# A hybrid decoder trunk: one part of layer 0's modulation summed on GpSimd during the state-space tiles

## The chip, the cores and the metric

The kernel runs on one core of a Trainium2 chip. Its engines work side by side, each through its own queue in order: TensorE (PE, with PEld for weight loads), VectorE (DVE), ScalarE (ACT), GpSimd (POOL) and SyncE (SP, which here only issues DMAs). They wait for one another through semaphores. The metric is the device time of one execution in microseconds, less is better.

## The reference

Two layers on a sequence of 256 tokens with 2048 channels. Each layer has a token mixer and a feed-forward part, and each of the two has three modulation vectors, made from one conditioning vector c:

```python
c_act = jax.nn.silu(c)
for i in range(DEPTH):
    mod = c_act @ ada_w[i] + ada_b[i]          # 2048 x (6 * 2048)
    sh_m, sc_m, gt_m, sh_f, sc_f, gt_f = [m[:, None, :] for m in jnp.split(mod, N_MOD, axis=-1)]
    h = x * (1.0 + sc_m) + sh_m
    y = s5_mixer(h, ...) if i % 2 == 0 else conv_mixer(h, ...)
    x = layer_norm(ALPHA * x + (1.0 + gt_m) * y, ln_g[i, 0], ln_b[i, 0])
    h = x * (1.0 + sc_f) + sh_f
    y = swiglu_ffn(h, ffn_w_gu[i], ffn_w_down[i])
    x = layer_norm(ALPHA * x + (1.0 + gt_f) * y, ln_g[i, 1], ln_b[i, 1])
```

Layer 0's mixer is a state-space scan (S5): 128 groups of 16 channels with 64 complex states each, then gelu and a gated projection with a 2048 x 4096 matrix. Layer 1's is a causal convolution between two projections. The six modulation parts of a layer are counted 0 to 5 below (sh_m, sc_m, gt_m, sh_f, sc_f, gt_f). Parts 0 and 1 of layer 0 are needed ahead of the scan, part 2 (the gate) when the mixer's output is added to x, parts 3 and 4 ahead of the feed-forward part, part 5 behind it. Each part is a product of c_act with 2048 rows of 2048 columns, 16 MB of weights.

## The kernel before

**Preparation** (0 to about 56 us): the scan's matrices are made, mostly on DVE and POOL.

**The state-space tiles** (about 56 to 254 us, the loop over ct in the kernel's function): 16 tiles of 128 channels. For tile ct, `tables` makes a table of powers (tile `tab`; two buffers): ACT copies the first half, POOL makes the second with four operations (`xt`, `yt`, two into `tab`, L350) from tile 2 on. `drive` brings the tile's input into a PSUM tile `pin` by matmuls (L413). `scan` on DVE multiplies `pin` by the table into `x` and `pin` (L430), scans (L442), carries the state over (L449 to L455), and turns back into `pc` and `psn` (L430). `read_out` makes y by 64 matmuls (L478). `gelu` is done in three steps between the scan's (DVE L1289, L1293, L1298; ACT), the last of which splits the result into a high and a low half, the low one on POOL (`h`, L1300). For every quarter of the tiles POOL also makes matrices ahead of time (`matrices`, L313: `mu`, `qb`, `qc`).

**Modulation blocks on PE** (`ada_block`, `ada_units`): in the first stage the modulation is made on PE. A block is one part and 512 columns; a unit is a quarter of it: one load of 1 MB on SP's queue into a buffer `raw`, and four matmuls (L605), whose total is turned (`adat`) and added up at the end of the block. Fourteen blocks, 56 units, go that way: parts 0 and 1, part 2, and the first half of part 3. The list `plan` says how many units go into each tile. Their order on PE is that of the code (`manual_schedule`); the other engines' order is set by a scheduler when the program is built. The buffers `raw` are five in this stage: four of the pool `rawp`, and one of a pool of its own.

**The rest of the modulation on DVE** (`AdaQueue`): from the end of the tiles on, DVE adds the rows of a part up itself: a 1 MB load `rawa`, then `acc = row * c_act[k] + acc` (L673, L675), and at the end of a part PE sums over the partitions (`total`, L683) and turns the result (`turned`). `rate` says how many steps fall to one weight unit of the dense part.

**The dense part** (from 254 us): gated projection, feed-forward, convolution, feed-forward. Weights of float32 are split into a high half (ACT, `whi`, L806) and a low half (DVE, `wlo`, L807), and PE multiplies (L856). `Later` puts small pieces of work off by a number of weight units. At the start of the gated projection, twelve `later.put` calls bring the units of `ada_block` that are left. The tail of tile 15 (`s5_end`) is done inside it.

Of the kernel before, what the change touches and what calls it, by code (L numbers as in the profile page):

```python
# [484 lines left out]
def kernel(  # L485
# [16 lines left out]
    def aux(name):  # L502
        return auxp.tile([P, 512], F32, tag="aux", name=name)
# [114 lines left out]

    class AdaQueue:
# [44 lines left out]
        def add(self, layer, j, b0, k, r):  # L664
            nb = 4 - b0
            rows, n = 4 // nb, 512 * nb
            if k == 0:
                self.acc = sp_ada.tile([P, D], F32, tag="adaacc", name="adaacc")
            acc = self.acc[:, :n]
            for i in range(rows):  # L670
                kk = rows * k + i
                if kk == 0:
                    nc.vector.tensor_scalar(out=acc, in0=r[:, 0], scalar1=c_act[:, 0:1], scalar2=None, op0=MUL)  # L673
                else:
                    nc.vector.scalar_tensor_tensor(out=acc, in0=r[:, i], scalar=c_act[:, kk:kk + 1], in1=acc, op0=MUL, op1=ADD)  # L675
            if kk < NCH - 1:
                return
            h = 32 * nb

            def total():  # L680
                ps = auxp.tile([P, 512], F32, tag="ada", name="adar", bufs=1)
                for b in range(nb):
                    nc.tensor.matmul(ps[32 * b:32 * b + 32, :], ones[:, 0:32], acc[:, 512 * b:512 * b + 512], start=True, stop=True)  # L683
                part = tp.tile([P, 512], F32, tag="adas", name="adas", bufs=1)
                nc.scalar.copy(out=part[:h], in_=ps[:h])
                later.put(1, lambda: turned(part))

            def turned(part):
                tr = aux("adat")
                for b in range(4):  # L690
                    nc.tensor.transpose(tr[:, b * h:(b + 1) * h], part[:h, b * P:(b + 1) * P], ident[:h, :h])
                nc.vector.scalar_tensor_tensor(
                    out=mod[layer][:, j, 4 * b0:].rearrange("p (b c) -> p c b", c=4),
                    in0=tr[:, :4 * h].rearrange("p (c b r) -> p c b r", b=nb, r=32)[:, :, :, 0],
                    scalar=plus_one(j), in1=ab_col[layer][:, 16 * j + 4 * b0:16 * j + 16].rearrange("p (b c) -> p c b", c=4),
                    op0=ADD, op1=ADD)

            later.put(1, total)


# [507 lines left out]
    parts = [(j, q) for q in range(4) for j in (0, 1)] + [(2, q) for q in range(4)] + [(3, 0), (3, 1)]  # L1208
# [108 lines left out]
    const2 = wp = ln_col = wtap = fold32 = row_of = None  # L1317
    with tc.manual_schedule(engines={mybir.EngineType.PE}):
        ada_units(3)
        for ct in range(-1, NCH):  # L1320
# [33 lines left out]
            while turns:  # L1354
                between()
    pin_ctx.close()
# [8 lines left out]
    ada = AdaQueue([(0, 3, 2), (0, 4, 0), (0, 5, 0)] + [(1, j, 0) for j in range(5)] + [(1, 5, 2)])  # L1365
# [43 lines left out]
    with mctx:  # L1409
        sp = mctx.enter_context(tc.tile_pool(name="s", bufs=1, reuse_waits="tile"))  # L1410
        sp_ada = mctx.enter_context(tc.tile_pool(name="ada", bufs=1, reuse_waits="tile"))
        stats = Stats("ln00", sp)
        ada.rate = 0.9
        for k in range(12):
            later.put(1 + k, lambda: ada_units(1))
# [14 lines left out]
        for i in range(8):  # L1430
# [6 lines left out]
            ada.hold = i == 6  # L1437
            if i == 0:
                later.put(10, load_vectors)
# [155 lines left out]
```

## Time and profile before

| what | value |
|---|---|
| median of 3 runs | 2387.75 us (2384.18 to 2388.4) |
| the profiled execution | 2382.7 us |
| its span | 2380.8 us |
| granted clock of TensorE, mean | 0.98 |
| busy: PE, DVE, ACT, POOL | 2279.4, 1665.8, 1021.3, 209.3 us |

The profile's page gives the span in 40 equal slices of 59.5 us. A digit is the busy share of a slice in tenths, PEclk the clock that TensorE was granted:

```profile
PE   5878899999999999999999999899999999999999
DVE  8999688787777677777985554788755444454564
POOL 4433000110000000000031111402000000000000
PEclk7998899999999999999999999999999999999999
```

The first four slices are the preparation and the state-space tiles, with DVE at 9 and PE at 8; the rest is the dense part, with PE at 9 throughout.

### The profile page before, as it was taken

The numbers are of one execution on the slowest core, as the hardware profiler recorded it, in microseconds if no ns is written. First come the engines' busy times: TensorE is split into PE (matmuls) and PEld (weight loads), VectorE is DVE, ScalarE is ACT, GpSimd is POOL, SyncE is SP. The second block draws the span as 40 slices with busy tenths as digits, with TensorE's granted clock in tenths as the row PEclk, the third lists the DMA queues.
The fourth block names the chain that finished last, engine by engine and source line by source line (L and its number), as shares of the span: only waits on it lengthen the run. The fifth ranks groups of instructions, "written<-read, shape, count | busy, mean of one in ns | idle before, by whom it ended". The sixth has DMA issues, their size and how long they took to land.

```text
span 2380.8 us, 34205 instructions
## 1 busy us (share of the span) xinstructions
PE 2279.4 (96%) x13997; PEld 1814.0 (76%) x13997; DVE 1665.8 (70%) x1850; ACT 1021.3 (43%) x1255; POOL 209.3 (9%) x217
## 2 busy tenths in 40 slices
PE   5878899999999999999999999899999999999999
PEld 2444588978888888888886677688888888888888
DVE  8999688787777677777985554788755444454564
ACT  3665233564343333433454332547343433334343
POOL 4433000110000000000031111402000000000000
PEclk7998899999999999999999999999999999999999
DMA  9877899678898889888744654675875555555542
GB/s 288 274 257 226 298 338 331 204 242 316 297 320 308 308 305 315 305 308 305 279 147 165 211 182 146 230 267 163 273 244 185 192 186 188 189 184 193 183 162 98
DMA packets 373330, 572.15 MB, mean 240 GB/s; under 512 B 17171, under 2 KB 267331, under 8 KB 358579
## 3 DMA queue, kind: packets, MB, share of 16 engines
q1 hardware_dynamic: 372742, 569.53, 70.5%
q8 instruction: 109, 1.79, 0.3%
q0 software_dynamic: 192, 0.37, 0.1%
q14 instruction: 47, 0.39, 0.0%
q10 hardware_dynamic: 240, 0.08, 0.0%
HBM read 567.83 MB, written 2.10 MB: 239 GB/s over the span
## 4 chain that ended last, share of the span: by engine, by line
PE 81%; DVE 9%; issue 5%; ACT 2%; POOL 2%; DMA 1%; DVEq 0%; SPq 0%; POOLq 0%; ACTq 0%
PE acc L856 69%; PE acc L860 4%; PE conv L1491 2%; PE turned L872 2%; PE spread L1481 1%; DVE pin L442 1%; POOL h L954 1%; PE y L478 1%; DVE x L430 1%; DVE pc L430 1%; DVE pin L430 1%; ACT whi L806 1%; DVE psn L430 1%; DMA raw<-in_ada_w_dram 1%; DVE wlo L807 1%
## 5 line engine op out<-in xcount | busy, mean ns | idle before, releaser
L807 DVE TENSOR_TENSOR wlo<-raw,whi 128x2048 fp32r<-128x2048 f32 x344 | 790.8, 2299 | 542.2 <-ACT whi L806 541.8
L806 ACT CAST whi<-raw 128x2048 fp32r<-128x2048 f32 x344 | 655.0, 1904 | 832.1 <-PE acc L856 608.8
L856 PE MATMUL acc<-whi,h 128*128 128x512 f32 x3648 | 900.4, 396 | 9.3 <-ACT whi L806 8.0
L856 PEld LDWEIGHTS acc<-whi,h 128*128 128x128 f32 x3648 | 681.1, 189 | 168.8 <-issue 11.5
L856 PE MATMUL acc<-wlo,h 128*128 128x512 f32 x1824 | 464.0, 391 | 1.0 <-DVE wlo L807 1.0
L856 PEld LDWEIGHTS acc<-wlo,h 128*128 128x128 f32 x1824 | 342.4, 188 | 76.8 <-DVE wlo L807 1.4
L856 PE MATMUL acc<-whi,f 128*128 128x512 f32 x1248 | 300.5, 391 | 0.0
L675 DVE SCALAR_TENSOR_TENSOR adaacc<-rawa,c_act,adaacc 128x2048 f32<-128x2048 f32 (+1 forms) x135 | 284.5, 2108 | 0.4
L856 PEld LDWEIGHTS acc<-whi,f 128*128 128x128 f32 x1248 | 233.0, 188 | 48.9 <-ACT whi L806 0.8
L856 PE MATMUL acc<-wlo,f 128*128 128x512 f32 x624 | 156.4, 389 | 0.0
L856 PEld LDWEIGHTS acc<-wlo,f 128*128 128x128 f32 x624 | 117.1, 188 | 24.3
L1470 POOL TENSOR_TENSOR lw<-fold,wtap 128x1024 f32<-128x1024 f32 x16 | 41.8, 2619 | 894.9 <-PE acc L860 710.5
L605 PE MATMUL ada<-raw,c_rep 128*32 128x512 f32 x512 | 75.0, 664 | 17.2 <-DMA raw<-in_ada_w_dram 17.2
L954 POOL TENSOR_TENSOR h<-hf,h 128x512 fp32r<-128x512 f32 x24 | 48.2, 2017 | 325.8 <-ACT h L953 318.6
L1179 ACT ACTIVATE fsg<-acc 128x256 f32<-128x256 f32 x84 | 31.9, 380 | 103.0 <-PE acc L856 102.9
L860 PEld LDWEIGHTS acc<-h,whi 128*128 128x128 f32 x512 | 61.1, 188 | 10.1 <-DVE h L1520 3.1
L860 PE MATMUL acc<-h,whi 128*128 128x256 f32 x512 | 65.1, 281 | 3.6 <-DVE h L1520 1.4
L1125 POOL CAST lnmh<-lno 128x2 fp32r<-128x2 f32 x1 | 0.2, 183 | 713.4 <-DVE lno L65 713.4
L1491 PE MATMUL conv<-vs,lw 128*32 128x256 f32 x1024 | 61.4, 381 | 0.0
L478 PE MATMUL y<-pc,mc 128*32 128x128 f32 x512 | 26.9, 322 | 26.6 <-DVE pc L430 26.6
L1491 PEld LDWEIGHTS conv<-vs,lw 128*32 128x32 f32 x1024 | 33.0, 110 | 25.2 <-issue 4.7
L1180 DVE TENSOR_TENSOR fsg<-acc,fsg 128x256 f32<-128x256 f32 x84 | 35.3, 420 | 19.9 <-ACT fsg L1179 19.8
(329 smaller groups left out, 1907.7 us busy)
## 6 DMA issues: line engine op xcount, KB each, us to landing
raw<-in_ffn_w_gu_dram SPq DMA_DIRECT2D x352, 512.0 KB, 4.5
rawa<-in_ada_w_dram SPq DMA_DIRECT2D x128, 1024.0 KB, 5.6
raw<-in_ffn_w_down_dram SPq DMA_DIRECT2D x88, 1024.0 KB, 5.2
raw<-in_ada_w_dram SPq DMA_DIRECT2D x64, 1024.0 KB, 7.1
raw<-in_s_w_glu_dram SPq DMA_DIRECT2D x64, 512.0 KB, 5.9
raw<-in_cv_w_pw_dram SPq DMA_DIRECT2D x64, 512.0 KB, 4.8
raw<-in_cv_w_pw_dram SPq DMA_DIRECT2D x16, 1024.0 KB, 6.3
X<-in_x_dram SPq DMA_DIRECT2D x8, 256.0 KB, 7.8
```

What stands on the lines that cost most here:

```text
L430: v.tensor_tensor(out=o, in0=i, in1=bc(t[:, k, a::2], 1, 4), op=MUL)
L478: nc.tensor.matmul(y[rr, o:o + HALF].rearrange("p (s c) -> p s c", s=2), self.cols(ct, ids[mi], p), src[:, p % 2, :, r, p // 2], start=Fal ...
L605: nc.tensor.matmul(acc[32 * k:32 * k + 32, :], c_rep[:, 4 * u + k, :], r[:, k, :], start=u == 0, stop=u == 3)
L675: nc.vector.scalar_tensor_tensor(out=acc, in0=r[:, i], scalar=c_act[:, kk:kk + 1], in1=acc, op0=MUL, op1=ADD)
L806: m1 = nc.scalar.copy(out=self.hi[:, :kn], in_=r[:, :kn])
L807: m2 = nc.vector.tensor_tensor(out=self.lo[:, :kn], in0=r[:, :kn], in1=self.hi[:, :kn].bitcast(F32), op=SUB)
L856: nc.tensor.matmul(acc[bank].rearrange("p a b -> p (a b)"), x[:, bank * HALF:(bank + 1) * HALF], wt[:, k], start=first, stop=end)
L860: nc.tensor.matmul(acc[bank][:, i], wt[:, k, m * P:(m + 1) * P], x, start=first and i == 0, stop=end and i == 1)
L872: nc.tensor.transpose(b[:, o:o + HALF], u[t][:, c0 + k * P:c0 + (k + 1) * P], ident)
L954: nc.gpsimd.tensor_tensor(out=hl[:, s2], in0=h, in1=hh[:, s2].bitcast(F32), op=SUB)
L1470: nc.gpsimd.tensor_tensor(out=lw, in0=fold32.unsqueeze(1).unsqueeze(1).broadcast_to([P, 4, CONV_G, 32]), in1=bc(wtap[:, :, 4 * ch:4 * ch + ...
L1491: nc.tensor.matmul(acc[32 * q:32 * q + 32, :], lw[:, q, g, :], vs[:, q, 4 * g:4 * g + SEQ], start=g == 0, stop=g == CONV_G - 1)
```

## The change

Part 2 (the gate) goes neither to PE nor to DVE now. A new class `Gate` has POOL add it up during the state-space tiles: in every tile one row block of 128 x 2048 (1 MB) is loaded by a DMA that POOL issues itself, into a buffer of `rawp`; POOL multiplies it by its column of c_act in place, and adds it to `gate` (the first one is written to `gate` at once). There are 16 of them. `gate.add()` and then `gate.load()` stand at the end of the loop's body, so a load stands one turn of the loop ahead of its addition. The fifth buffer for blocks is given up; its room holds `gate`. PE's 56 units go to parts 0, 1, 3 and the first half of 4. DVE's queue begins at the second half of part 4, 16 rows shorter, and begins only after the first of the eight gated projections (rate 0 there, then 0.6 instead of 0.9); the units left over from the tiles begin at the fifth weight unit instead of the first. The final sum over the partitions (`total`, `turned`) becomes a function `column_sums`, which both use. `gate_end` does it for the gate.

```diff
-    parts = [(j, q) for q in range(4) for j in (0, 1)] + [(2, q) for q in range(4)] + [(3, 0), (3, 1)]
+    parts = [(j, q) for q in range(4) for j in (0, 1)] + [(3, q) for q in range(4)] + [(4, 0), (4, 1)]
...
+    class Gate:
+        def __init__(self, acc):
+            self.k, self.held, self.acc = 0, [], acc
+
+        def load(self):
+            if self.k < NCH:
+                r = rawp.tile([P, 4, 512], F32, tag="raw", name="rawg").rearrange("p a b -> p (a b)")
+                nc.gpsimd.dma_start(r, ada_w[0, self.k * P:(self.k + 1) * P, 2 * D:3 * D])
+                self.held.append((self.k, r))
+                self.k += 1
+
+        def add(self):
+            if self.held:
+                k, r = self.held.pop(0)
+                nc.gpsimd.tensor_scalar(out=r if k else self.acc, in0=r, scalar1=c_act[:, k:k + 1], scalar2=None, op0=MUL)
+                if k:
+                    nc.gpsimd.tensor_tensor(out=self.acc, in0=r, in1=self.acc, op=ADD)
...
-    raws[:] = [rawp] * 4 + [more.enter_context(tc.tile_pool(name="raw5", bufs=1))]
+    gate = Gate(more.enter_context(tc.tile_pool(name="gate", bufs=1, side="right")).tile([P, D], F32, name="gate"))
...
-                    raws[:] = [rawp]
-                    more.close()
                     s5.keep_ctx.close()
...
             while turns:
                 between()
+            gate.add()
+            gate.load()
...
-    ada = AdaQueue([(0, 3, 2), (0, 4, 0), (0, 5, 0)] + [(1, j, 0) for j in range(5)] + [(1, 5, 2)])
+    ada = AdaQueue([(0, 4, 2), (0, 5, 0)] + [(1, j, 0) for j in range(5)] + [(1, 5, 2)])
...
-        sp_ada = mctx.enter_context(tc.tile_pool(name="ada", bufs=1, reuse_waits="tile"))
-        ada.rate = 0.9
+        gate_total, gate_turned = column_sums(0, 2, 0, gate.acc)
+
+        def gate_end():
+            nonlocal sp_ada
+            gate_total(aux("adar"))
+            later.put(2, gate_turned)
+            more.close()
+            sp_ada = mctx.enter_context(tc.tile_pool(name="ada", bufs=1, reuse_waits="tile"))
+
+        later.put(1, gate_end)
         for k in range(12):
-            later.put(1 + k, lambda: ada_units(1))
+            later.put(5 + k, lambda: ada_units(1))
...
             ada.hold = i == 6
+            ada.rate = 0.6
```

The scheduler sets where the new operations stand on POOL. Before, this stood in POOL's queue around the tables of tiles 7 to 9 (the number behind `tab` is the tile, `h` is the low half of a gelu):

```order
L1300 TENSOR_TENSOR h_132<-gl_1519,h_132 128x256
L350 TENSOR_TENSOR xt_1578<-tab7_1576,wt_363 128x256
L350 TENSOR_TENSOR yt_1579<-tab7_1576,wt_363 128x256
L350 TENSOR_TENSOR tab7_1576<-xt_1578,yt_1579 128x4x32 x2
L1300 TENSOR_TENSOR h_132<-gl_1674,h_132 128x256
L350 TENSOR_TENSOR xt_1728<-tab8_1726,wt_363 128x256
L350 TENSOR_TENSOR yt_1729<-tab8_1726,wt_363 128x256
L350 TENSOR_TENSOR tab8_1726<-xt_1728,yt_1729 128x4x32 x2
```

In the changed kernel, from the ninth load on (`rawg` is the gate's buffer, L1318 its load, L1325 the scaling and L1327 the addition), the same engine does:

```order
L1318 DMA rawg_1890<-in_ada_w_dram 128x2048
L1305 TENSOR_TENSOR h_132<-gl_1700,h_132 128x256
L1325 TENSOR_SCALAR rawg_1890<-rawg_1890,c_act_125 128x2048
L1327 TENSOR_TENSOR gate_486<-rawg_1890,gate_486 128x2048
L350 TENSOR_TENSOR xt_1758<-tab8_1756,wt_363 128x256
L350 TENSOR_TENSOR yt_1759<-tab8_1756,wt_363 128x256
L350 TENSOR_TENSOR tab8_1756<-xt_1758,yt_1759 128x4x32 x2
L1318 DMA rawg_2058<-in_ada_w_dram 128x2048
L1305 TENSOR_TENSOR h_132<-gl_1862,h_132 128x256
L1325 TENSOR_SCALAR rawg_2058<-rawg_2058,c_act_125 128x2048
L1327 TENSOR_TENSOR gate_486<-rawg_2058,gate_486 128x2048
L350 TENSOR_TENSOR xt_1929<-tab9_1927,wt_363 128x256
```

Between two tables there stand a load, the scaling that waits for this load, and the addition; a load is issued behind the addition of the load before it. In other tiles (3, 5, 6, 10, 14) the tables stand between the load and the scaling.

On PE the end of the tiles before (`y` is the read-out of tiles 14 and 15, L605 are modulation units):

```order
L413 MATMUL pin<-uh,lz_455 128x2x64 x8
L612 MATMUL adat<-ident,adas 128x128 x4
L605 MATMUL ada<-raw,c_rep 32x512 x4
L468 MATMUL y<-u,bd_458 128x129
L605 MATMUL ada<-raw,c_rep 32x512 x8
L478 MATMUL y<-pc,mc_453 32x128 x16
L478 MATMUL y<-psn,mc_453 32x128 x16
L605 MATMUL ada<-raw,c_rep 32x512 x4
```

and after the change (L627 and L634 are the gate's sum over the partitions and its transposes):

```order
L413 MATMUL pin<-uh,lz_455 128x2x64 x8
L612 MATMUL adat<-ident,adas 128x128 x4
L605 MATMUL ada<-raw,c_rep 32x512 x4
L468 MATMUL y<-u,bd_458 128x129
L627 MATMUL adar<-gate,ones 32x512 x4
L634 MATMUL adat<-ident,adas 128x128 x4
L468 MATMUL y<-u,bd_456 128x129
L478 MATMUL y<-pc,mc_453 32x128 x16
L478 MATMUL y<-psn,mc_453 32x128 x16
L605 MATMUL ada<-raw,c_rep 32x512 x4
```

The gate's total stands ahead of the read-out of tile 14, and three modulation units less stand ahead of the dense part; they follow inside it.

More of the change, by code (lines that the diff above doesn't have):

```diff
@@ L677, in add @@
                 return
[L678 to L698, printed above, removed]
+            total, turned = column_sums(layer, j, b0, acc)
+            later.put(1, lambda: (total(auxp.tile([P, 512], F32, tag="ada", name="adar", bufs=1)), later.put(1, turned)))
     def inverse_std(v, y, hv, t):
@@ L1315, in start_dense @@
             ready.append(Unit(wp, s5_w_glu[0], 4 * u, 4, [(0, 256), (D, 256)]))
-    const2 = wp = ln_col = wtap = fold32 = row_of = None
+    const2 = wp = sp_ada = ln_col = wtap = fold32 = row_of = None
     with tc.manual_schedule(engines={mybir.EngineType.PE}):
```

19 lines of the change are left out of this document (added).

## The prediction

> **What bounds the kernel now.** I read the time by stages first (busy time of each engine in each stretch), then VectorE's groups in the first stage, then single tiles on the timeline.
>
> ```profile
> 60.00:235.00 175.00, 140.42 (x2133) 80.94 (x2135) 165.35 (x358) 110.87 (x318) 64.47 (x113) 0.92 0.76 253
> 235.00:260.00 25.00, 14.84 (x114) 9.39 (x106) 19.29 (x31) 1.69 (x4) 0.72 (x1) 0.61 0.97 328
> 260.00:300.00 40.00, 39.67 (x231) 29.45 (x230) 25.45 (x22) 14.67 (x14) 1.27 (x1) 1.00 0.83 278
> 300.00:440.00 140.00, 140.00 (x704) 115.66 (x703) 121.56 (x118) 60.03 (x61) 0.00 (x0) 1.00 0.92 316
> 500.00:1180.00 680.00, 680.00 (x3092) 557.27 (x3091) 517.35 (x365) 270.58 (x215) 0.00 (x0) 1.00 0.87 308
> ```
>
> Columns: stretch, length, busy us of PE, weight load, DVE, ACT, POOL (with counts), granted clock, DMA share, GB/s. Two machines stand one behind the other. From 60 to 235 us, the state-space tiles, DVE is busy 165 of 175 us and PE is not full. From 260 on PE is full, at a granted clock of 1.00, while DVE has room (517 of 680 us). So the 16 column additions that the change takes from DVE's modulation queue in the dense part buy nothing there: PE sets that time. What the change can win or lose lies ahead of 260 us.
>
> ```profile
> L442 DVE TENSOR_TENSOR_SCAN pin<-rho,pin 128x256 f32<-128x256 f32 x60 | 41.4, 689 | 0.8
> L430 DVE TENSOR_TENSOR x<-pin,tab 128x512 f32<-128x512 f32 x32 | 21.3, 679 | 5.0 <-PE pin L413 5.0
> ```
>
> VectorE's groups of the tile stage: 32 products x for 16 tiles, with 5.0 us idle once, at the start. One tile costs DVE about 12 us. Its first product reads the tile's table (tab), and this table comes from POOL:
>
> ```profile
> 210.62 1.28 DVE L430 TENSOR_TENSOR x<-pin,tab 128x512 f32<-128x512 f32 x2
> 217.90 0.68 DVE L430 TENSOR_TENSOR x<-pin,tab 128x512 f32<-128x512 f32 x1
> 222.05 1.28 DVE L430 TENSOR_TENSOR psn<-pin,tab 128x512 f32<-128x512 f32 x2
> 228.22 0.68 DVE L430 TENSOR_TENSOR x<-pin,tab 128x512 f32<-128x512 f32 x1
> ```
> ```profile
> 218.43 0.73 POOL L1300 TENSOR_TENSOR h<-gl,h 128x256 fp32r<-128x256 f32 x1 [4.05 <-ACT h L1299]
> 223.97 0.61 POOL L350 TENSOR_TENSOR xt<-tab,wt 128x256 f32<-128x256 f32 x1 [4.80 <-ACT tab L358]
> 224.54 0.61 POOL L350 TENSOR_TENSOR yt<-tab,wt 128x256 f32<-128x256 f32 x1
> 225.23 0.88 POOL L350 TENSOR_TENSOR tab<-xt,yt 128x128 f32<-128x128 f32 x2
> 226.05 0.88 POOL L1378 DMA_DIRECT2D rt<-in_cv_w_dw_dram  x1
> ```
>
> The timeline of tiles 13 to 15. Tile 13's psn ends at 223.3 and frees a table buffer, tile 15's table is done at 226.1, and x of tile 15 starts at 228.2. So the table has **2.1 us of slack**, though POOL idles 4 to 5 us ahead of each of its jobs. Idle POOL is not free POOL: what is put there must not be in the way when the table falls due.
>
> **The change, part by part.** *POOL* gets per tile a 1 MB load that it issues itself, a scaling (tensor_scalar, 128x2048) and an addition (tensor_tensor, 128x2048). Neither shape is in the trace. The nearest rows:
>
> ```profile
> L313 POOL TENSOR_TENSOR qc<-mu,mu x12: 720/728/902, 51.3 to 126.4; 128x256 f32<-128x256 f32 x12
> L1530 POOL TENSOR_TENSOR hf<-hf,V x7: 1272/1293/3330, 1506.1 to 1528.8; 128x512 f32<-128x512 f32 x7
> L1470 POOL TENSOR_TENSOR lw<-fold,wtap x16: 1966/2066/4020, 1203.7 to 1467.8; 128x1024 f32<-128x1024 f32 x16
> masks.py:199 POOL TENSOR_SCALAR_AFFINE_SELECT ident<-ident 128x128 f32<-128x128 f32 x1 | 0.3, 295 | 0.1
> L189 POOL MEMSET mb<- 128x512 f32 x2 | 1.1, 535 | 0.0
> ```
>
> Addition: from 728 ns at 256 to 1293 at 512 is 565 ns for 256 elements, so 1293 + 6 x 565 = 4.7 us at 2048; doubling the 1024 row's minimum gives 3.9. I take **4.6** (range 3.9 to 4.7). Scaling has one input: four 512 memsets are 2.1 us (no input at all), the 128-element select gives 16 x 295 = 4.7 with its fixed part counted sixteen times. By the slope of a two-input operation (565/256 = 2.2 ns) a 128-element one has some 0.45 us, the select 0.3, so one input costs about half: **2.3** (range 1.8 to 4.7).
>
> ```profile
> raw<-in_ada_w_dram SPq DMA_DIRECT2D x37, 1024.0 KB, 5.9
> rt<-in_cv_w_dw_dram POOLq DMA_DIRECT2D x1, 128.0 KB, 8.3
> ```
> ```profile
> DMA to landing us min/median/max: 4.8/5.6/8.6
> ```
>
> Landing of a load: 1 MB from SP's queue takes 5.9 us in these tiles, from POOL's queue even 128 KB took 8.3; the last row is rawa, 1 MB in the same rows of 8 KB, over the whole run. POOL's issue occupies it for 0.88 us. I take **6.5** from issue to landing (range 4.8 to 8.3).
>
> Now the order. In the changed order POOL does for tile 8, in a row: issue load 8, h, scale 8, add 8, tables of tile 8, issue load 9, h, scale 9, and so on. Load 9 is issued behind add 8, and scale 9, which waits for that load, stands ahead of the tables of tile 9. So the landing is not hidden behind earlier work; it is a wait in the middle of POOL's queue, and behind it stand tables for which DVE waits. Per tile of this form: 6.5 + 2.3 + 4.6 + 2.1 (tables: 0.61 + 0.61 + 0.88) = **15.5 us against DVE's 12**. In tiles where the tables stand inside the landing it is 13.4 and a little.
>
> The whole chain on POOL, counted off its new order from the issue of load 0 to the tables of tile 15: 15 landings that nothing else on POOL fills (load 2's is filled by an addition and a table), 16 scalings, 14 additions (the last is behind the last table), and what doesn't lie in a landing: tables 16.8, seven h of 0.7 = 4.9, nine matrix operations (0.6 to 0.7 each) 5.8, one issue 0.9; together 28.4. The prices of the matrix operations, and the start:
>
> ```profile
> 109.57 1.43 POOL L313 TENSOR_TENSOR qb<-mu,mu 128x256 f32<-128x256 f32 x2
> 110.95 2.37 POOL L313 TENSOR_TENSOR mu<-cm,par 128x256 f32<-128x256 f32 x4
> ```
> ```profile
> 56.97 2.35 POOL L313 TENSOR_TENSOR mu<-cm,par 128x256 f32<-128x256 f32 x4
> ```
>
> Load 0 is issued behind the last row, at 59.3. The sum is 15 x 6.5 + 16 x 2.3 + 14 x 4.6 + 28.4 = 97.5 + 36.8 + 64.4 + 28.4 = 227.1, so tile 15's table is done at 286.4 instead of 226.1: **60.3 us later**. DVE's own 16 x 12 = 192 us are shorter than the chain and lie beside it.
>
> *The end of the tiles* gets some of it back.
>
> ```profile
> 231.07 2.27 DVE L807 TENSOR_TENSOR wlo<-raw,whi 128x2048 fp32r<-128x2048 f32 x1
> 243.81 1.27 DVE L673 TENSOR_SCALAR adaacc<-rawa,c_act 128x1024 f32<-128x1024 f32 x1
> 245.60 1.25 DVE L675 SCALAR_TENSOR_TENSOR adaacc<-rawa,c_act,adaacc 128x1024 f32<-128x1024 f32 x1
> 248.70 1.27 DVE L675 SCALAR_TENSOR_TENSOR adaacc<-rawa,c_act,adaacc 128x1024 f32<-128x1024 f32 x1
> 253.02 1.28 DVE L430 TENSOR_TENSOR psn<-pin,tab 128x512 f32<-128x512 f32 x2
> ```
>
> Before, tile 15 ended at 254.2, 28.1 us behind its table, with four of the modulation's operations (5 us), two wlo of 2.3 and PE's waits for the last blocks among its work. In the new order there is no adaacc among it, and one wlo: x and the rest of tile 14 take 5.2 us, wlo 2.3, tile 15 itself some 10.5, and y of tile 14 comes 1 to 2 us late, because PE's new total of the gate column (4 matmuls and the transposes) stands ahead of it and waits for the last addition. That is 19.5 us, so 8.6 us are won: 60.3 - 8.6 = 51.7.
>
> *TensorE.* Its 56 blocks stay 56, but three more of the seven last ones fall behind the tiles, where PE is full, and one total of the old queue leaves there.
>
> ```profile
> 229.54 1.06 PE L605 MATMUL ada<-raw,c_rep 128*32 128x512 f32 x8
> ```
>
> 3 x 1.06 less one total of about 1 us: +2. *SP* has four buffers for blocks and gate rows where it had five for blocks, and some block loads now wait for POOL's addition; a tile of 15 us leaves the 5.9 us landing room, so I cost that at nothing. If the tiles were short it would count (below). *Later*: the smaller rate and the shorter queue leave PE's dense work as it is, 0.
>
> Sum: 51.7 + 2 = **+54 us**. The profiled execution took 2382.7 us (span 2380.8), so 2436 like for like; the runs' median is 2387.75, 5 above it, so their median would be near 2441. I predict 2440. At the low ends of landing, scaling and addition the sum is 72 + 29 + 55 + 28 = 184 and the whole +9 to +11 (2395); with landing 8.3 and the slow scaling it is 124 + 75 + 64 + 28 = 292, and +119 (2504). All ends at once are unlikely, so I go in from both.
>
> The Trainium skill, "DMA: Bandwidth & Descriptors", section on the anatomy of a gpsimd DMA, fits such a transfer by 2.0 us plus its bytes at 436 GB/s, which for 1 MB is an estimate of 4.4 us. With it the chain would be 32 us shorter and the time near 2409. The row of POOL's queue above (8.3 us for 128 KB) disagrees with it, since other loads ran beside; no run here shows 1 MB from that queue.
>
> **The rivals.**
> *POOL fits in the gaps, and the tiles stay DVE's (faster).* POOL was idle for 110 of 175 us, which speaks for it. Then only the end of the tiles counts: 8.6 us won, 2 lost, 2381 for the runs. It decides from the point where landing + scaling + addition + tables come to 12 us or less: with 2.1 for tables and at the least 1.8 + 3.9 the landing would have to be 4.2 us, below the 4.8 us minimum of rawa. Against it also the slack of 2.1 us. 6%.
>
> *DMA becomes the bound of the tiles.* In those 175 us they moved 253 GB/s, 44 MB; 16.8 MB more are 61 MB, at the 328 GB/s of the stretch behind 185 us. That is 10 us more, less 6.6 at the end: 2391, about no change. It needs POOL's chain to be short as well. 6%.
>
> *The chain, and DVE's own operations are held up by POOL's long ones.*
>
> ```profile
> 112.65 0.68 DVE L452 TENSOR_TENSOR cx<-cx,cy 128x4 f32<-128x4 f32 x1
> 113.26 0.15 DVE L453 TENSOR_TENSOR cx<-cx,cy 128x4 f32<-128x4 f32 x1
> ```
>
> The first of these equal, tiny operations ran while POOL did its mu of 0.59 each (110.95 to 113.3), and took 0.68 instead of 0.15: it waited for the end of one. Beside an addition such a wait is up to 4.6 us. In tiles of 15 us it falls into DVE's new idle time; in the five whose tables stand early (3, 5, 6, 10, 14) it doesn't, at most 5 x 4.6 = 23 us: 2463. The Trainium skill, "SBUF — State Buffer", section on who interferes with whom, says that a VectorE instruction with two SBUF inputs and a GpSimd instruction that reads SBUF exclude each other for a whole instruction. By that rule the wait scales with POOL's instruction; the two rows agree for 0.6 us, longer ones aren't in the trace. 13%.
>
> **How the numbers follow.** The chain as summed has 75%, with its uncertain prices 2405 to 2475; the held-up form 13%; the two short forms 12%. The range goes from 2405 to 2480. Within 0.2% (about 5 us, what a measurement can tell from no change) lie most of the second rival and the edges of the others: 5%; faster by more: the better part of the first, 5%; slower 90%.
>
> **What would show it.** After the change the tile stage should last some 52 us longer; DVE should wait at x (tab from POOL) for 30 us and more in all, POOL's idle time should stand ahead of the scalings with the gate's DMA as its releaser, at 5 us and more each, and from 260 + 52 on everything should be as before. If POOL's idle time is ahead of the tables (ACT tab) as now, and DVE is busy through the tiles, I am wrong about the order; if the scaling takes over 4 us or the landing under 5, only about the size.

## The result, and the profile after

| what | before | after |
|---|---|---|
| median of 4 runs each | 2387.97 us (2384.18 to 2388.4) | 2505.85 us (2501.3 to 2506.83) |
| ratio, 95% interval | | 1.0497 (1.0480 to 1.0514) |
| span of the profiled execution | 2380.8 us | 2505.0 us |
| table of tile 15 done | 226.1 us | 348.0 us |
| last psn of tile 15 ends | 254.3 us | 370.5 us |

The change makes the kernel 118 us slower. The forecast, 2440, has the right sign and the right place, but the time lies 66 us above it and outside its range. Below, times of single runs are compared with 2505.85. Runs of one kernel lie up to 9 us apart here, so 5 us between two single runs say nothing.

The stages of the changed kernel (stretch, length, busy us of PE, weight load, DVE, ACT, POOL, granted clock, DMA share, GB/s):

```profile
60.00:350.00 290.00, 156.32 (x2116) 89.96 (x2112) 186.85 (x351) 108.93 (x316) 219.52 (x148) 0.75 0.59 207
350.00:371.00 21.00, 11.01 (x120) 5.72 (x120) 20.25 (x31) 4.00 (x6) 11.36 (x14) 0.58 0.83 231
630.00:1310.00 680.00, 680.00 (x3122) 557.77 (x3120) 516.09 (x372) 268.73 (x213) 0.00 (x0) 1.00 0.87 307
```

The tiles take 290 us where they took 175. DVE, busy 165 of 175 before, is now busy 187 of 290. POOL has become the busiest engine, 220 of 290, and DMA moves 207 GB/s where it moved 253, so it isn't the bound. The last row is a stretch of the dense part, 130 us later than the one of before: PE is full, 680 of 680, as before. Nearly all of the loss is ahead of it.

The groups of POOL's new operations and of DVE's first product in a tile, and the gate's loads (the last column of a group is the idle time ahead of it and what ended it; of the load row, KB and the median us from issue to landing):

```profile
L1325 POOL TENSOR_SCALAR rawg<-rawg,c_act 128x2048 f32<-128x2048 f32 x15 | 81.5, 5435 | 60.8 <-DMA rawg<-in_ada_w_dram 60.8
L430 DVE TENSOR_TENSOR x<-pin,tab 128x512 f32<-128x512 f32 x32 | 21.4, 684 | 84.1 <-POOL tab L350 78.9
L1327 POOL TENSOR_TENSOR gate<-rawg,gate 128x2048 f32<-128x2048 f32 x15 | 67.9, 4525 | 0.7
...
rawg<-in_ada_w_dram POOLq DMA_DIRECT2D x16, 1024.0 KB, 7.7
```

The prices are there to be read: scaling 5.43 us (I took 2.3), addition 4.53 (4.6), landing, from a load's issue until its data are there, 7.7 (6.5). POOL idles 60.8 us ahead of scalings, waiting for the row that it has just asked for (67.5 with the first), and DVE waits 78.9 us for tables.

POOL's timeline in tiles 14 and 15:

```profile
322.64 5.43 POOL L1325 TENSOR_SCALAR rawg<-rawg,c_act 128x2048 f32<-128x2048 f32 x1 [6.06 <-DMA rawg<-in_ada_w_dram]
328.16 4.55 POOL L1327 TENSOR_TENSOR gate<-rawg,gate 128x2048 f32<-128x2048 f32 x1
332.66 0.73 POOL L1305 TENSOR_TENSOR h<-gl,h 128x256 fp32r<-128x256 f32 x1
333.34 0.60 POOL L1318 DMA_DIRECT2D rawg<-in_ada_w_dram  x1
333.97 0.62 POOL L350 TENSOR_TENSOR xt<-tab,wt 128x256 f32<-128x256 f32 x1
334.55 0.61 POOL L350 TENSOR_TENSOR yt<-tab,wt 128x256 f32<-128x256 f32 x1
341.74 5.43 POOL L1325 TENSOR_SCALAR rawg<-rawg,c_act 128x2048 f32<-128x2048 f32 x1 [6.58 <-DMA rawg<-in_ada_w_dram]
347.16 0.85 POOL L350 TENSOR_TENSOR tab<-xt,yt 128x128 f32<-128x128 f32 x2
```

Tile 15's table needs 2.1 us of work. It begins at 333.97 and is done at 348.0, because a wait for a row and that row's scaling stand between its second and its third operation.

### The profile page after: what moved, and what is told of

Read it like the earlier page. It is cut to its first block, busy times and chain, and to the rows that moved or that the text cites. A ratio compares the mean times of both kernels' runs of the same rounds, so it can differ in the third digit from the quotient of the medians.

```text
span 2505.0 us, 34207 instructions
## 1 busy us (share of the span) xinstructions
PE 2302.9 (92%) x13997; PEld 1827.4 (73%) x13997; DVE 1660.5 (66%) x1834; ACT 1021.6 (41%) x1255; POOL 373.1 (15%) x264
## 5 line engine op out<-in xcount | busy, mean ns | idle before, releaser
L699 DVE SCALAR_TENSOR_TENSOR adaacc<-rawa,c_act,adaacc 128x2048 f32<-128x2048 f32 (+1 forms) x120 | 249.5, 2079 | 5.4 <-DMA rawa<-in_ada_w_dram 5.1
L605 PE MATMUL ada<-raw,c_rep 128*32 128x512 f32 x512 | 81.9, 721 | 57.6 <-DMA raw<-in_ada_w_dram 57.6
L1325 POOL TENSOR_SCALAR rawg<-rawg,c_act 128x2048 f32<-128x2048 f32 x15 | 81.5, 5435 | 60.8 <-DMA rawg<-in_ada_w_dram 60.8
L430 DVE TENSOR_TENSOR x<-pin,tab 128x512 f32<-128x512 f32 x32 | 21.4, 684 | 84.1 <-POOL tab L350 78.9
L1327 POOL TENSOR_TENSOR gate<-rawg,gate 128x2048 f32<-128x2048 f32 x15 | 67.9, 4525 | 0.7
```

Source lines behind the costliest of these rows:

```text
L605: nc.tensor.matmul(acc[32 * k:32 * k + 32, :], c_rep[:, 4 * u + k, :], r[:, k, :], start=u == 0, stop=u == 3)
L1325: nc.gpsimd.tensor_scalar(out=r if k else self.acc, in0=r, scalar1=c_act[:, k:k + 1], scalar2=None, op0=MUL)
L1327: nc.gpsimd.tensor_tensor(out=self.acc, in0=r, in1=self.acc, op=ADD)
```

## The experiments

Two theories came out of the prediction. **S**: POOL's queue is one serial sum of landings, scalings, additions and tables, and my error is in its prices. **V**: VectorE's own operations are held up by POOL's long ones. A third, **B**, came up on the way: the gate's rows take buffers from the ring that TensorE's block loads use.

### What each part of the chain is worth

Run e1 takes the multiplication out of rows 1 to 15, run e9 makes it as dear as I had priced it, and run e15 does it with another instruction:

```diff
-   nc.gpsimd.tensor_scalar(out=r if k else self.acc, in0=r, scalar1=c_act[:, k:k + 1], ...)
+e1    if k == 0: (the same)
+e9    n = 768 if k else D;  nc.gpsimd.tensor_scalar(out=r[:, :n] ..., in0=r[:, :n], scalar1=c_act[:, k:k + 1], ...)
+e15   nc.gpsimd.tensor_tensor(out=r if k else self.acc, in0=r, in1=c_act[:, k:k + 1].broadcast_to([P, D]), op=MUL)
```

> Leaves out the multiplication of part 2's rows by their column, in 15 of 16 rows; loads and additions stay. Theory S (POOL's queue is one serial chain of landing, scaling, addition and tables, and the mis-sized term is the scaling, 5.43 us and not 2.3): the chain loses 15 x 5.43 = 81 us, table 15 is done near 267 instead of 348, the kernel takes 2420 to 2430. Rival L (the landings, longer than I took them, are the larger part): the landing waits grow into the time that goes free, because each load still has to wait for other loads; less than 50 us are won, over 2455. Rival V (VectorE's own operations are held up by POOL's long ones, whatever POOL's order): the wait falls by about half, 55 us, near 2450, and VectorE's groups at L350 and L452 stay as long as now.

> The scalings behind row 0 work on 768 of 2048 columns (the other columns of part 2 stay unscaled), which by run e2's 64 columns (0.44 us) and 2048 (5.43) is 2.2 us: the price that my prediction had for the whole. Loads, additions and order stay. If the mis-sized scaling is the step that failed: the chain loses 15 x 3.2 = 48 us, so 2450 to 2465, near the 2440 that I gave (what is left are 15 landings of 7.7 instead of 6.5, 18 us, and the dense part, 7). Rival (in e1 the removal of 81 us won only 63, because VectorE's waits at y and its held-up operations take the place of waits for the table): in the same proportion 37 us are won, 2465 to 2475. If the scaling isn't the cause: over 2480.

> The scaling as a tensor_tensor with the column spread out along the row (a second input with step 0) instead of a tensor_scalar with a column operand; the same numbers. If the price of a POOL operation went by its inputs, as I took it (one input half of two), this would be slower: 2510 or more. If POOL reads the column operand anew for each element, a tensor_tensor at the addition's 3.6 to 4.5 us is shorter than 5.43: 16 x 0.9 to 1.8 = 14 to 29 us off the chain, 2477 to 2492.

Measured: e1 2443.06, e9 2471.24, e15 2476.73. The scaling rows of e9 and then of e15:

```profile
L1326 POOL TENSOR_SCALAR rawg<-rawg,c_act 128x768 f32<-128x768 f32 x15 | 33.1, 2207 | 64.3 <-DMA rawg<-in_ada_w_dram 64.3
```
```profile
L1325 POOL TENSOR_TENSOR rawg<-rawg,c_act 128x2048 f32<-128x2048 f32 x15 | 54.0, 3600 | 51.0 <-DMA rawg<-in_ada_w_dram 51.0
```

In e15 the scalings take 16 x 1.83 = 29 us less of POOL and the kernel 29 us less of time, one to one. It is the cleanest of the three: up to the last table the scheduler left POOL's order as it is in the changed kernel, so that only the price differs, and table 15 is done at 318.9 instead of 348.0, 29 us earlier too. In e9 a scaling at 2.2 us, my price, gives 2471: **the wrong price is worth 35 us of the 66**, though the order of some tables changed with it. That is less than the 48 us taken from POOL, as the rival in e9 had it, and e1's 63 us are less than its 81, a time that none of the three had (V's "near 2450" is the nearest): as POOL gets faster, other waits come in. The groups of e1 show them (DVE's first product, and its wait for y of the tile before):

```profile
L430 DVE TENSOR_TENSOR x<-pin,tab 128x512 f32<-128x512 f32 x32 | 21.4, 681 | 18.3 <-POOL tab L350 13.5 <-PE pin L413 4.8
L1294 DVE SCALAR_TENSOR_TENSOR y<-u,vec,y 128x256 f32<-128x256 f32 x16 | 7.7, 482 | 25.5 <-PE y L478 25.5
```

The wait for tables is down from 78.9 to 13.5, but DVE now waits 25.5 us for y (17.6 in the changed kernel), and its held-up operations (the next part) are probably on the path; no run takes them out of e1.

Run e2 shrinks the operations to 64 columns, e3 takes the loads away, e4 leaves rows 1 to 15 out altogether:

```diff
+e2    n = 64 if k else D      (scaling and addition on [:, :n])
+e3    r = rawp.tile(...) if self.k == 0 else self.acc     (a DMA for row 0 only)
-   if self.k < NCH:
+e4    if self.k < 1:
```

> The 15 scalings and additions behind row 0 work on 64 of 2048 columns (part 2 is left incomplete); loads, their waits and the order stay. Theory S: the chain is 288 - 15 x (5.43 + 4.53) + about 15 x 0.6 = 148 us, shorter than VectorE's 192 us, so the tiles are VectorE's again: 2380 to 2395. Rival L: the landing in the middle of POOL's queue alone holds the tables up, over 2420. Rival V: without long operations on POOL nothing is held up, also 2380 to 2395, so this run does not tell S and V apart, the next one does.

> Only row 0 is loaded; the other 15 scalings and additions work on the accumulator itself (part 2 is another number), so POOL computes as much as in the changed kernel but waits for no landing. Theory S: the chain is 288 - 15 x 7.7 = 172 us plus short waits for ScalarE's copies, close to VectorE's 192: 2385 to 2415. Rival V: VectorE's operations beside POOL's 5 us ones are held up in nearly all tiles, so most of the loss stays, over 2450. Rival L: everything was the landing, 2380.

> Only row 0 of part 2 is loaded and scaled, the other 15 rows are left out altogether; all else of the change stays (blocks of parts 3 and 4, four raw buffers, late start, rates, total of the columns). This is the change without its chain. Theory S as I priced the rest: end of the tiles -8.6, TensorE +2: 2381, -6 us. Rival (the parts that I cost at nothing, above all three units and the later queue in the dense part, cost more; the trace of the changed kernel shows that stretch 7 us longer): 2386 to 2392.

Measured: e2 2416.56, e3 2493.62, e4 2391.63. So the chain costs 114 us of the 118, and the rest of the change 4, which is no more than the spread of single runs. E2 lies between its expectations, near L's lower end. POOL still idles 69.6 us for landings (62.1 and 7.5), but only 25 us over e4 remain: the wait alone, without the 10 us of work behind it, fits for the larger part into a tile. E3's time is the one expected of V. Its stages say something else: the scheduler, which had no load to place, put nearly all rows into the first half.

```profile
60.00:245.00 185.00, 71.17 (x974) 41.28 (x970) 102.28 (x158) 49.85 (x148) 177.12 (x93) 0.70 0.38 131
245.00:333.00 88.00, 71.31 (x1108) 42.20 (x1112) 81.97 (x182) 54.13 (x161) 23.04 (x41) 0.91 0.68 228
```

POOL is busy 177 of 185 us while DVE is busy 102, and then DVE 82 of 88 while POOL is busy 23: full one behind the other, not side by side. So 2493 is the price of an order, and the run doesn't separate S from V.

### Is VectorE held up by long POOL operations?

```diff
+e11   for q in range(4):  s = slice(512 * q, 512 * q + 512);  (scaling and addition on [:, s])
```

> Every scaling and addition in four pieces of 512 columns; the same work, nothing is computed otherwise. Theory V' (a VectorE operation on two SBUF inputs stands still until POOL's current instruction ends): VectorE's excess at L350, L452 and L615 (23 us in all in the changed kernel; xq 5.0 us a piece against 0.9) shrinks with the piece, to under 8 us, xq under 2 us. If instead VectorE is slowed in proportion to POOL's busy time, the excess stays near 23 us. The kernel's time: POOL's chain gets 60 x some 0.1 us longer; little is won where VectorE waits for tables anyway: 2495 to 2515.

Measured: 2530.44. Operations of DVE on small or short tiles, of the changed kernel and then of e11:

```profile
L350 DVE TENSOR_TENSOR tq<-xq,yq 128x256 f32<-128x256 f32 x4 | 11.9, 2969 | 0.0
L350 DVE TENSOR_TENSOR xq<-tq,wt 128x512 f32<-128x512 f32 x2 | 10.0, 5019 | 0.0
L452 DVE TENSOR_TENSOR cx<-cx,cy 128x4 f32<-128x4 f32 x16 | 8.4, 528 | 0.3
```
```profile
L350 DVE TENSOR_TENSOR tq<-xq,yq 128x256 f32<-128x256 f32 x4 | 2.9, 718 | 0.0
L350 DVE TENSOR_TENSOR xq<-tq,wt 128x512 f32<-128x512 f32 x2 | 1.4, 708 | 0.0
L452 DVE TENSOR_TENSOR cx<-cx,cy 128x4 f32<-128x4 f32 x15 | 4.4, 294 | 0.3
```

With the two other groups that are hit (yq at L350, and L615) they take 40.2 us in the changed kernel, 11.8 before, and 18.3 in e11: the excess goes from 28.4 to 6.5 us when the same work comes in pieces of a quarter. So V's mechanism is real, and over all groups it shrinks with the length of a POOL instruction, as expected. L615 alone does not follow: 7.6 us in the changed kernel, 7.3 in e11. Its longest one in e11, and POOL beside it:

```profile
153.59 3.07 DVE L615 SCALAR_TENSOR_TENSOR mod<-adasum,adab 128x4 f32<-128x4 f32 x1
```
```profile
153.80 0.61 POOL L350 TENSOR_TENSOR yt<-tab,wt 128x256 f32<-128x256 f32 x1
154.37 0.72 POOL L313 TENSOR_TENSOR qb<-mu,mu 128x256 f32<-128x256 f32 x1
155.05 0.86 POOL L350 TENSOR_TENSOR tab<-xt,yt 128x128 f32<-128x128 f32 x2
155.88 0.71 POOL L313 TENSOR_TENSOR qb<-mu,mu 128x256 f32<-128x256 f32 x1
```

It takes 3.07 us and ends, to 0.1 us, with the last of these, though no POOL instruction there is longer than 0.72. So it looks as if a row of short ones without a gap can hold DVE up as well, and the expectation of e11, that DVE waits for the end of the current instruction only, is not the whole of it. The kernel does not get faster for the 22 us that DVE wins. POOL's pieces cost 22 us more in all (177.1 against 154.8; the groups of e11 below), far more than I had put down, and the kernel takes 24.6 us more, all of POOL's 22. That fits DVE's hold-ups lying, in the changed kernel, in time in which it would wait for a table anyway.

```profile
L1327 POOL TENSOR_SCALAR rawg<-rawg,c_act 128x512 f32<-128x512 f32 x60 | 94.5, 1585 | 67.6 <-DMA rawg<-in_ada_w_dram 67.6
L1331 POOL TENSOR_TENSOR gate<-rawg,gate 128x512 f32<-128x512 f32 x60 | 76.4, 1296 | 0.0
```

### Who waits for the row

Runs e7 and e8 put the scaling on ScalarE; e5 and e8 keep GpSimd's queue in the order of the code; e10 asks for one more row ahead:

```diff
+e5,e8 with tc.manual_schedule(engines={mybir.EngineType.PE, mybir.EngineType.Pool}):
+e7,e8 nc.scalar.activation(out=r if k else self.acc, in_=r, func=AF.Copy, scale=c_act[:, k:k + 1])
+e10   if gate.k == 1: gate.load()      (behind gate.load())
```

> The changed kernel with GpSimd's instructions of the tile stage in the order in which the code states them (tables, h, matrices, scaling, addition, then the load of the next row), where the scheduler had put the load directly ahead of the scaling that waits for it. Nothing is computed otherwise. Theory S+ (serial chain on POOL; the order puts the landing in it): the landings now lie beside tables, h and matrices, so the 67 us of POOL's idle time ahead of scalings go; what is left is 16 x (5.43 + 4.53 + 0.6) + 28 + waits for ScalarE's copies = some 205 us of POOL against VectorE's 192: table 15 done near 275, the kernel at 2420 to 2445. Rival B (the raw buffers that the rows hold keep SP's block loads back, and y comes late): little is won, over 2470, and TensorE's waits at ada for raw stay near 48 us.

> The 16 scalings on ScalarE (a 128x2048 operation takes 1.9 us there) instead of GpSimd; nothing is computed otherwise. Theory S: like e1_no_scaling (2443) plus at most 16 x 1.9 where the addition waits for it: 2443 to 2470, if ScalarE's queue isn't held up by the landing. Rival: ScalarE stands behind the wait for the landing and with it the copies for tables, weights and gelu; then up to 16 x 6 us are added: over 2480.

> Both: scalings on ScalarE and GpSimd's queue in the order of the code. Nothing is computed otherwise. Theory S+: POOL has 4.53 + 0.6 + 3.8 = 9 us of work per tile against VectorE's 12, and no landing in the middle: no wait of VectorE for tables, 2391 (run e4) + up to 15 for VectorE's operations held up by additions = 2391 to 2410. Rival B: blocks are still late by the shared buffers: 2410 to 2425.

> Each row of part 2 is loaded one step earlier (two rows under way), nothing is computed otherwise. Theory S: POOL's idle time ahead of scalings (67 us) nearly goes, POOL is full with its 215 us of work, table 15 is done near 290 instead of 348, the kernel at 2440 to 2455. Rival B (rows hold a second one of four raw buffers): SP's block loads wait longer, TensorE waits at ada for more than 48 us and y is late, over 2470. If POOL's compute were not the bound behind the landings, the tiles would go back to VectorE's 192 us: under 2415.

Measured: e5 2494.13, e7 2443.24, e8 2525.23, e10 2497.85. E7 equals e1 to 0.2 us: moved to ScalarE, the scaling is as good as gone from POOL. E8, which I expected to be the best, is the slowest of the four. In it ScalarE's longest waits in the tiles are these (us in total, times, longest):

```profile
ACT rawg L1325 <- DMA rawg<-in_ada_w_dram: 94.3, 14, 13.3
ACT rho L364 <- DVE pin L442: 44.5, 9, 8.7
```

The landing has not gone; ScalarE's queue waits for it, and behind that stand the copies for the next tile's input and gelu. In e5 POOL's idle time for rows falls from 67.5 to 26.0 us, but POOL waits 31 us for h and for a table's copy instead, most of it at the start; 12 us are won. Its numbers are those that I had put down for B: over 2470, and TensorE waits 49 us for blocks. Run e17 below shows that late blocks are not what holds e5 back: there TensorE waits 74 us for blocks, and the kernel is 19 us faster than e5. In e10 the edit didn't get through: from the fifth row on the scheduler put each load ahead of its own scaling again, behind the addition, so it tests neither theory.

Three more runs shorten the landing itself, by loading 512 of 2048 columns, and one pins GpSimd's order with the load one tile ahead (tables, load, h, matrices, scaling of the row before, addition):

```diff
+e13   (on e1) load [:, :512]; the addition reads it four times over
+e16   load [:, :512]; scaling of columns 512 to 2047 out of it, then of the first 512
+e17   manual_schedule for Pool; gate.load() behind s5.tables(ct + 1); scaling in the two pieces of e16; full loads
+e18   e17 with the loads of e16
```

> Run e1 (no multiplication behind row 0) with only the first 512 of 2048 columns of rows 1 to 15 loaded (256 KB) and added four times over, so the additions are as large as before (part 2 is another number). Theory S: with the scaling gone, the landings are what is left of the chain: table 15 follows 15 times the change in landing. If a landing is 2 to 3 us shorter, the chain of e1 (227 us from load 0) falls to VectorE's 192 plus what holds VectorE up (20 us), and the kernel goes from 2443 to 2400 to 2415. Rival V (VectorE held up by additions of 4.5 us is what e1 still loses): the additions are the same, so the time stays over 2430.

> The changed kernel with only the first 512 of 2048 columns of rows 1 to 15 loaded (256 KB, which landed in 4.9 us in run e13 instead of 7.7), and scaled into the other columns from there, so that GpSimd scales (in two pieces, 1536 and 512, by the other runs 4.1 + 1.6 us) and adds as much as in the changed kernel; part 2 is another number. Theory S (the landings count 15 times, as summed): 15 x 2.8 = 42 us less, 15 x 0.3 more, 2465 to 2475. If landings don't count so (in e13 3 us less moved the table by 8 us only), 2485 to 2500.

> GpSimd's order pinned in every tile: tables of the next tile, load of a row, h, matrices where there are any, scaling (in two pieces as in run e16), addition; full loads of 1 MB, nothing computed otherwise. It is the base for e18. Theory S: POOL's sum with the landing in it in every tile, as in the changed kernel: 2490 to 2530.

> The same order, instruction by instruction, as in e17, with loads of 256 KB (512 of 2048 columns of rows 1 to 15, scaled into the others; part 2 is another number). Only the landing differs, 2.5 to 2.8 us a row. Theory S (the landing counts in POOL's sum wherever nothing fills it): 20 to 40 us below e17. Rival (another wait takes its place, as in e13 and e16: h from ScalarE, y, VectorE): 0 to 12 us below e17.

Measured: e13 2441.23, e16 2510.23, e17 2475.38, e18 2480.66. My expectation for e17 was wrong, in a useful way: with the load fixed a tile ahead of its use, POOL never waits for a row. One of the shortest tiles of e17:

```profile
254.74 0.62 POOL L350 TENSOR_TENSOR xt<-tab,wt 128x256 f32<-128x256 f32 x1
255.31 0.62 POOL L350 TENSOR_TENSOR yt<-tab,wt 128x256 f32<-128x256 f32 x1
256.00 0.87 POOL L350 TENSOR_TENSOR tab<-xt,yt 128x128 f32<-128x128 f32 x2
256.81 0.61 POOL L1318 DMA_DIRECT2D rawg<-in_ada_w_dram  x1
257.45 0.74 POOL L1305 TENSOR_TENSOR h<-gl,h 128x256 fp32r<-128x256 f32 x1
258.16 4.16 POOL L1326 TENSOR_SCALAR rawg<-rawg,c_act 128x1536 f32<-128x1536 f32 x1
262.32 1.55 POOL L1328 TENSOR_SCALAR rawg<-rawg,c_act 128x512 f32<-128x512 f32 x1
263.96 4.54 POOL L1330 TENSOR_TENSOR gate<-rawg,gate 128x2048 f32<-128x2048 f32 x1
268.46 0.61 POOL L350 TENSOR_TENSOR xt<-tab,wt 128x256 f32<-128x256 f32 x1
```

No row has idle time ahead of it; here the period, 268.46 - 254.74 = 13.7 us, is POOL's work alone, against DVE's 12. **The landing in POOL's queue, with the order that puts it there, is worth 30 us** (2505.85 - 2475.38), although the scalings are 5 us dearer in two pieces.

Over all tiles of e17 POOL is still the busiest engine, 237 of 272 us, with 29 us of waits for h. But it no longer holds DVE up by its tables. DVE's waits for TensorE and for tables, and SP's longest wait (us in total, times, longest):

```profile
DVE y L1294 <- PE y L478: 25.8, 7, 5.4
DVE x L430 <- PE pin L413: 12.4, 4, 4.8
DVE x L430 <- POOL tab L350: 3.3, 1, 3.3
```
```profile
SPq L562 <- POOL gate L1330: 116.1, 12, 14.8
```

SP, which loads TensorE's blocks, waits 116 us for additions on POOL, each of which sets a row's buffer free, and TensorE waits 74 us for blocks. By these waits, what DVE waits for in e17 comes by the path of B. How much of the 84 us by which e17 still stands above e4 this is stays open: no run has this order and a buffer of its own for the rows.

E18's loads are shorter and nobody waits for them: no gain, outside both of its expectations. So e18 did not test the size of the landing. E16 and e13 didn't either. In e16 the landing falls to 5.2 us but POOL's idle time for rows only from 67.5 to 55.6, since the scheduler moved tables out of the gap; h then waits, and the time stays (2510, above both expectations). E13 won 2 us, no more than the spread, where S expected 28 and more and V expected a time over 2430. That DVE's hold-ups, 16.5 us there, count once the scaling is gone would explain it, but is not shown. What 1.2 us less of landing would bring at the same order was not measured.

### Buffers, and the late start of the queue

```diff
+e6    (on e2) raw pool of 3 for the blocks, a pool of 1 for the rows
+e12   (on the kernel before) ada.rate = 0.0 in the first dense unit, then 0.9
+e14   (on e4) ada.rate = 0.9 from gate_end on, 0.6 from the third unit
```

> Run e2_landing_only (64 of 2048 columns scaled and added, part 2 left incomplete), with the four raw buffers divided: three for TensorE's blocks, one for the rows of part 2. Its e2 stood 25 us above e4. Rival B (the rows in the shared ring keep SP's block loads back: SP waited 101 us for rows to land, TensorE 21.6 us for blocks, VectorE 20.1 us for y): SP's wait for rows goes, VectorE's wait for y falls from 20 to near 5, 2391 to 2400. Theory L (the landing in POOL's queue holds tables and h up: 6.4 and 5.5 us of waits): stays at 2410 to 2420, VectorE still waits at y.

> The kernel before with one number changed: VectorE's modulation queue begins after the first dense unit (rate 0 in it, then 0.9 as before), so that its first four operations (5 us of VectorE) no longer stand in the end of tile 15. All else is the kernel before. By run e4 the end of the tiles was 6.6 us shorter without them: dense would begin up to 5 us earlier, 2380 to 2385 against 2387 to 2388, if the queue still keeps its due time; rival: DMA stands idle at the start of the dense part and the queue's loads fall together with the weights later, TensorE waits there: 2387 to 2393.

> Run e4 (rows 1 to 15 of part 2 left out, 2391.6 in one look) with VectorE's modulation queue begun as soon as its buffer exists, in the first dense unit, at rate 0.9, and 0.6 from the second. If the late start of the queue is what made the dense part 7 to 10 us longer (DMA idle in its first 20 us, full at 313 to 333 us, where TensorE waits): about 6 us better, 2383 to 2387, as the kernel before. If the three block units that moved into the dense part are it (3.2 us, and their transposes): stays at 2389 to 2393.

Measured: e6 2444.34; e12 2390.23, ratio to the kernel before 1.0020 (1.0009 to 1.0031); e14 2397.87, 1.0046 (1.0032 to 1.0060). For B, e2 shows the coupling:

```profile
SPq L562 <- DMA rawg<-in_ada_w_dram: 101.1, 14, 12.1
```
```profile
DVE y L1294 <- PE y L478: 20.1, 9, 9.0
DVE x L430 <- POOL tab L350: 6.4, 2, 5.8
```

SP's queue stands 101 us behind rows that have not landed, blocks come late, y comes late, and DVE waits for y longer than for tables (4.4 us for y in e4). With its own buffer for rows, e6's wait for y is 6.4 us, but the scheduler packed the rows into the early tiles, tables came late there (32.7 us), and the time got worse than either expectation. So the coupling is seen in the waits, and its price in time stays open.

E12 and e14 look for a gain in VectorE's queue and find none: beginning it late costs the kernel before 0.2%, and beginning it early does not help e4 (e14 is above both of its expectations). No run beat the kernel before. Even with the chain gone for nothing, e4, the change is at 2391.6, no faster than before.

## Why the prediction was wrong

**What bounds the kernel**: right. The dense part is unchanged where PE is full, and 16 additions taken from DVE there bought nothing.

**The order, and the chain that it makes**: right. POOL's idle time stands ahead of the scalings with the gate's DMA as releaser, 14 times and 4.8 us on average (I asked for 5 and more each), and DVE waits at x for POOL's table, 78.9 us where I asked for 30 and more.

**The price of the scaling, 2.3 us: the step that failed.** It is 5.43. I reasoned that one input costs half of two, from a 128-element select and a memset; there was no row of that operation, and the upper end of my own range, 4.7, was still too low. Nor did my two rows give a half: the select's 0.3 us against the 0.45 worked out for a two-input operation is two thirds, which would have been 3.1. In the sum the error is 16 x 3.1 = 50 us; put at my price (e9) it gives back 35 us of time, and the part of it that e15 takes away at an unchanged order, 29 us, comes back in full. The Trainium skill, "GPSIMD Engine Reference", section on engine selection, says that GpSimd is about half as fast as VectorE in two-input operations and roughly at line rate in one-input ones. Here the operation with one full input and a column was the slower one, 5.43 against 4.53 us.

**The landing, 6.5 us**: also too low, 7.7 (5.1 to 9.4; the 4.4 us of the fit that the prediction quotes lies below all of them). In the sum that is 15 x 1.2 = 18 us; no run shows what this difference alone is worth in time. With the measured prices the sum is 15 x 7.7 + 16 x 5.43 + 14 x 4.53 + 28.4 = 294 us, and the trace has 348.0 - 59.9 = 288. As a sum it holds to 2%; e13 and e16 show that its terms aren't independent of the order, and that a landing which is made shorter need not come back as time.

**The addition, 4.6**: right (4.53). **The end of the tiles, 19.5 us behind the table**: 22.5, 3 us short.

**TensorE and the dense part, +2**: from the end of tile 15 to the end of the span it is 2134.5 us where it was 2126.5, so +8. Part of it lies in the gated projection. The first and the last operation on fsg, before and after:

```profile
L1179 ACT ACTIVATE fsg<-acc x84: 372/380/386, 496.9 to 2246.2; 128x256 f32<-128x256 f32 x84
```
```profile
L1184 ACT ACTIVATE fsg<-acc x84: 372/382/386, 618.3 to 2368.5; 128x256 f32<-128x256 f32 x84
```

Counted from the end of tile 15 it takes 242.6 and 247.8 us to the first, so 5 more; three moved units at 1.06 us each and their transposes are near that. In e14, with the queue early, the 5 us stay too, so the late start isn't needed to explain them; but in e4 the same stretch is 9 us longer behind a tile 15 that ends at 250.6, so the split between the two stages isn't sharp and the cause of this part stays open.

Together: table 15 is 61.6 us later than predicted (121.9 against 60.3), the end of the tiles 3 longer, the dense part 6 longer: 70.6, and the span is 70.5 above the 2434.5 of my sum. The range failed by its top: I had worked out 2504 for dear scaling and slow landing together, called it unlikely and cut it off at 2480. Both came. That 2504 lies so near the 2505.85 is partly luck: the scaling was dearer than its upper end, the landing shorter, and 9 us come from the last two terms.

**The rivals.** POOL fitting in, and DMA as the bound: refuted (290 us, 207 GB/s). The hold-up of VectorE: its mechanism is there (28.4 us in all), and e11 speaks against its being on the path in the changed kernel; in e1 and e13, where POOL has less to do, it probably is. The rule of the Trainium skill, "SBUF — State Buffer", section on who interferes with whom, that such a pair excludes each other for a whole instruction, agrees with e11 in the sum: quarter pieces, 6.5 us instead of 28.4. The one hold-up of 3.07 us across several short instructions in e11 is longer than any of them. **SP and the four buffers, costed at nothing**: wrong as a reason. I took a longer tile for cover; e2 shows SP waiting 101 us behind the rows. In the changed kernel the tables are later still, so little of it can show; in e17, where the tables are in time, DVE waits 38 us for TensorE and 3 for a table.

## What to carry to other kernels

An operation that waits for a load should be issued far enough behind it on its own queue; e17 won 30 us with such an order. Giving the wait to another in-order engine can go either way: with the scaling on ScalarE e7 won 63 us, and e8, with POOL's order pinned besides, lost 19. Where the trace has no row for an operation, a bound from a different kind of operation is a guess: price the work by its slowest relative, knowing that even this can be too low, and don't trim the range where two such guesses add. And if the scheduler sets the order, an edit that changes a duration can change the order too (in e9 it did, in e15 it did not): read the new order before reading the new time, or pin it.

## What was not expected of the hardware

- GpSimd's `tensor_scalar` with a column operand takes 0.44 us for 64 columns, 1.55 for 512, 2.20 for 768 and 5.43 for 2048: some 2.5 ns an element, for one input. The same product as a `tensor_tensor` with the column as a second input of step 0 takes 3.60 us, a third less. Two different full rows take 4.53, and in e3 one full row read as both inputs 3.60.
- A DVE operation on 128x4 elements, next to a POOL addition in the changed kernel, took 3.57 us. The groups L615 and L452 have such cases:

```profile
347.98 4.49 POOL L1327 TENSOR_TENSOR gate<-rawg,gate 128x2048 f32<-128x2048 f32 x1
```
```profile
348.92 3.57 DVE L615 SCALAR_TENSOR_TENSOR mod<-adasum,adab 128x4 f32<-128x4 f32 x1
```

It ends with the addition, at 352.5; where nothing holds it up it takes 0.15 us.
